# A latent-attention encoder layer on one core: gates of a folded weight and sums of normalised rows are moved to the steps that hold the value products

## The chip, the cores and the metric

The kernel runs on one core of a Trainium2 chip, as one launch. The metric is the time of the launch on the device in microseconds (us). Three runs of the kernel before took 2022.31, 2024.96 and 2029.78 us, with a median of 2024.96 us. One further execution was recorded by the hardware profiler. It took 2024.07 us.

The engines are named as in the profile: PE multiplies matrices, PEld loads its weights, DVE and POOL are the two vector engines, ACT computes activations and copies, SP issues transfers (SPq is its queue).

## The reference

One encoder layer is applied to two sequences of 1024 rows by 1024 columns, `prompt` and `sample`, each with its own conditioning vector. Everything is float32.

```
mod = silu(c) @ w_ada + b_ada            # shift, scale, gate for both halves
h   = rmsnorm(x, g_mix) * (1 + sc1) + sh1
z   = h @ w_in                           # 256 query latents, 128 kv latents, 64 rope, 512 Fourier
p   = softmax((q_nope k_nope + q_pe k_pe) / sqrt(192));  o = p v      # 4 heads
mix = concat(o, fourier(f_in)) @ w_out
x   = x + ga1 * mix
h2  = rmsnorm(x, g_ffn) * (1 + sc2) + sh2
y   = rmsnorm(x + ga2 * ((silu(h2 @ w_gate) * (h2 @ w_up)) @ w_down), g_final)
```

The output is y for both sequences.

## The kernel before

Every product that must keep float32 precision is made of three matmuls: each operand is split into a high part (`hi`, a rounded copy made by ACT, line 63) and a low part (`lo = x - hi`, made by DVE, line 64), and `mm3` (lines 79 to 81) adds hi*hi, hi*lo and lo*hi. So a tensor can be used by PE only after one ACT and one DVE instruction have split it.

The program runs in stages: projections of both sequences into latents and Fourier inputs, a Fourier stage, the attention stage (from 300 to about 716 us in the profile), and the feed-forward stage, which fills the rest. The change lies in the attention stage only.

**The steps.** The attention stage is a loop over k = 0 to 63, one step for each of 2 sequences (s), 4 blocks of 256 rows (b), 4 heads (h) and 2 halves (u) of a block. Steps 0 to 31 belong to sequence 0, steps 32 to 63 to sequence 1. Step k issues:

- `scores` (line 1221): ten matmuls into a PSUM pair, DVE's row maximum `mx` (line 1238), ACT's exponential into `p` (line 1243), DVE's reciprocal and the scaling of `p` (line 1245). The 64 rows of line 1238 in the profile are the 64 steps, and the one numbered k is the start of step k's softmax.
- in steps with k % 8 = 3 and 4, `rope_q` (line 849) for the next block of rows: matmuls, three DVE products `qt` (lines 860 to 862), one POOL sum (863), and the copies `qsk` by ACT and DVE (865, 866).
- in steps with k % 4 = 1 from 5 on, `values` (line 1261): 24 matmuls of the probabilities of four earlier steps with the kv latents, and one split of the result.
- `flip_p` (line 1249) of step k - 1: PE transposes `p` into two PSUM banks `ppt` (line 1258), and ACT and DVE split each bank into `pt`. PE can write a bank again only when both have read it.
- from step 10 to 57, `out_step` (line 1204) for a block finished earlier. Every second step adds an output projection `out_proj` (line 1170) of 12 matmuls against the folded weight `wv`, with a DVE sum (1177). Of each eight, two steps (k % 8 = 4 and 0) end with `norm2` (line 1179). That is a root mean square by ACT (1185), a chain of six small POOL instructions (104 to 111) and a DVE scaling `xn` (1187). Two steps transpose the normalised rows (`flip_h`) and store them to `h2_d`.
- at its end, whatever stands in the table `todo[k]` (lines 1310 to 1328).

**What stands in the table.** The output projection needs the folded weight `wv`, multiplied by the gate `ga1` of the sequence. It is 4 heads by two halves of 512 columns, so eight tiles of 128 x 512. `wv_load` loads them raw. `wv_gate(i)` (line 1299) multiplies tile i by the gate on POOL, in place. `wv_split(i)` (line 1304) splits it on ACT and DVE into `wv`. Tiles 0 to 3 are the first half of the columns, tiles 4 to 7 the second. `gate_half` loads 512 columns of the gate, in a tile with one buffer. So the second half's gate can be loaded only when tiles 0 to 3 are multiplied. All this is done twice: for sequence 0 before step 10 (first half) and step 12 (second half), and for sequence 1 before steps 42 and 44, once sequence 0's last projections are done.

`comb_h(0, c)` (line 1278), for c = 0 to 3, loads four 128 x 512 tiles of sequence 0's normalised rows into `hca`, makes four sums and differences of them on POOL into `hcb`, and stores those to `hc_d` for the feed-forward stage. `hca` and `hcb` have one buffer each. `add_x(i)` (line 821) issues a transfer from POOL's queue that adds a piece of x to a partial result in DRAM. Ahead of it a tiny POOL sum (827) waits for the reciprocal of the step.

**What sets the order.** The program text gives the order of importance. The framework's planner then orders each engine's queue from its own estimate of when each instruction is ready, and an instruction written later can be queued ahead of one that is not ready. The text pins an instruction behind another one on the same engine with `tc.issue_after`. `wv_gate` and `comb_h` are pinned behind `here["p"]`, which is the last POOL instruction of the latest `rope_q` or `norm2` written before. `wv_split` is pinned by `behind()` to the latest split written before. Loads are not pinned: the load for the first combination is written in step 49, whose maximum starts at 617.09 us, and it was issued at 584.28 us. The hardware then runs each queue in order, each instruction when what it waits for has happened.

Of the kernel before, what the change touches and what calls it, by code (L numbers as in the profile page):

```python
# [53 lines left out]
def hybrid_encoder_kernel(ctx: ExitStack, tc: tile.TileContext, a: dict):  # L54
# [7 lines left out]
    def split(hi, lo, src, eng=None):  # L62
        here["a"] = nc.scalar.copy(hi, src).ins  # L63
        here["v"] = (eng or nc.vector).tensor_tensor(out=lo, in0=src, in1=rd(hi), op=ALU.subtract).ins  # L64
# [6 lines left out]
    def behind():  # L71

        st = ExitStack()
        st.enter_context(tc.issue_after(here["a"]))
        st.enter_context(tc.issue_after(here["v"]))
        return st
# [841 lines left out]
    with ExitStack() as st:  # L918
# [180 lines left out]
        for s in range(2):  # L1099
            for t in range(8):  # L1100
# [26 lines left out]
                if s == 0:  # L1127
# [7 lines left out]
                    if t in (4, 6):  # L1135
                        c = t // 2 - 2
# [78 lines left out]
    with ExitStack() as st:  # L1215
# [58 lines left out]
        def gate_half(s, g):  # L1274
            S["ga"] = e.tile([P, 512], F32, tag="gah", name="gah")
            nc.sync.dma_start(S["ga"], ga_d[32 * g + s, :].partition_broadcast(P))

        def comb_h(s, c):
            A = e.tile([P, 4, 512], F32, tag="lat00", name="hca")
            B = e.tile([P, 4, 512], F32, tag="lat01", name="hcb")  # L1280
            for i in range(2):
                nc.sync.dma_start(A[:, 2 * i : 2 * i + 2, :], h2_d[s][:, c + 4 * i, :].rearrange("p (a b) -> p a b", a=2))
            a11, a21, a12, a22 = (A[:, i, :] for i in range(4))
            with tc.issue_after(here["p"]):
                add(B[:, 0, :], a21, a22, nc.gpsimd)
                sub(B[:, 1, :], B[:, 0, :], a11, nc.gpsimd)
                sub(B[:, 2, :], a11, a21, nc.gpsimd)
                sub(B[:, 3, :], a12, B[:, 1, :], nc.gpsimd)
                nc.gpsimd.dma_start(hc_d[s][:, c], B)
# [9 lines left out]
        def wv_gate(i):  # L1299
            h, g = i % 4, i // 4  # L1300
            with tc.issue_after(here["p"]):
                nc.gpsimd.tensor_tensor(out=S["wv", h, g], in0=S["wv", h, g], in1=S["ga"], op=ALU.mult)

        def wv_split(i):
            h, g = i % 4, i // 4
            gs = slice(512 * g, 512 * g + 512)
            with behind():
                split(wv[0][:, h, gs], wv[1][:, h, gs], S.pop(("wv", h, g)))

        todo = {k: [] for k in range(nit)}  # L1310
# [5 lines left out]
                todo[33].append(lambda: gate_half(1, 0))  # L1316
            todo[33 + g].append(lambda g=g: wv_load(1, g))
        for i in range(8):
            todo[39 + i // 2].append(lambda i=i: wv_split(i))
            todo[34 + i // 2].append(lambda i=i: wv_gate(i))  # L1320
            todo[(4, 4, 5, 5, 6, 6, 7, 7)[i]].append(lambda i=i: wv_gate(i))
            if i == 3:
                todo[5].append(lambda: gate_half(0, 1))
                todo[35].append(lambda: gate_half(1, 1))
            todo[6 + i // 2].append(lambda i=i: wv_split(i))
        for c, k in enumerate((49, 51, 57, 59)):
            todo[k].append(lambda c=c: comb_h(0, c))
        for i, k in enumerate((6, 8, 10, 12, 17, 18, 19, 25, 26, 27, 33, 34, 35, 41, 42, 43)):
            todo[k].append(lambda i=i: add_x(i))
# [3 lines left out]
        for k in range(nit + 4):  # L1333
            if k >= nit:
                i = k - nit
# [7 lines left out]
            if k < nit:  # L1343
# [3 lines left out]
                i = k % 8  # L1347
# [657 lines left out]
```

## Time and profile before

| | |
|---|---|
| runs, us | 2022.31, 2024.96, 2029.78 |
| median of the runs, us | 2024.96 |
| profiled execution, us | 2024.07 |
| span of its instructions, us | 2022.3 |
| PE busy in the span, us | 1972.9 (98%) |
| DVE / ACT / POOL busy, us | 1390.8 / 891.4 / 827.1 |
| mean granted clock of PE | 0.997 |
| attention stage, 300 to 716 us: PE busy of 416.00 us | 410.35 |

The span runs from the first to the last instruction of the profiled execution; its time is 1.77 us longer. A row of a timeline gives the start of an instruction in us from the start of the span, its duration in us, the engine, the line of the program, the operation, the tile written and the tiles read, shapes, and in brackets how long the engine was idle before it and what ended that. Where a row has a count over 1 at its end, the duration is that of the whole group. A row of a table by stretches gives, for each engine, busy time and instructions in brackets, then PE's clock, the share of the DMA engines and GB/s.

### The profile page before, as it was taken

To read this page: it belongs to the slowest core of one execution; us is meant where nothing else is said; L and a number is where in the kernel's file an instruction comes from. 1 tells how busy PE (TensorE), PEld (TensorE's weight loads), DVE (VectorE), ACT (ScalarE), POOL (GpSimd) and SP (SyncE) were. 2 spreads that over 40 slices of the span, in tenths; PEclk is the share of its full clock that TensorE was granted. 3 is DMA by queue.
4 is the path that set the end of the run, shared out by engine and by line. 5 is a ranking of instruction groups with operands and counts; after the bars stand their busy time and mean duration, and the time that the engine had idled before them with its cause. 6 is when DMAs were issued, how large, how long until landed. Compare 5 with 4: busy or idle time off the path is not lost.

```text
span 2022.3 us, 27551 instructions
## 1 busy us (share of the span) xinstructions
PE 1972.9 (98%) x9526; PEld 1618.1 (80%) x9526; DVE 1390.8 (69%) x2060; ACT 891.4 (44%) x1716; POOL 827.1 (41%) x972
## 2 busy tenths in 40 slices
PE   6899999999999999999999999999999999999998
PEld 3788778888888877888888888877888888888876
DVE  4568758666777679678778587688655655657674
ACT  2675436555565564333333365453333333336451
POOL 0564212111413237878878411234544544410142
PEclk9999999999999999999999999999999999999999
DMA  9786884445544376555555597674322322358662
GB/s 386 268 320 208 288 311 108 128 91 137 128 115 146 136 265 207 184 187 193 183 180 193 163 312 250 224 229 156 135 88 100 119 91 103 113 186 280 217 224 94
DMA packets 183033, 376.59 MB, mean 186 GB/s; under 512 B 17996, under 2 KB 57548, under 8 KB 179052
## 3 DMA queue, kind: packets, MB, share of 16 engines
q1 hardware_dynamic: 165548, 321.33, 47.1%
q0 software_dynamic: 17344, 53.49, 9.2%
q8 instruction: 75, 1.23, 0.3%
q14 instruction: 66, 0.54, 0.1%
HBM read 262.75 MB, written 120.39 MB: 189 GB/s over the span
## 4 chain that ended last, share of the span: by engine, by line
PE 55%; DVE 3%; DMA 2%; issue 1%; POOL 1%; ACT 0%; SPq 0%; DVEq 0%; ACTq 0%; POOLq 0%
PE bank L80 18%; PE bank L79 18%; PE bank L81 18%; DVE wl L64 1%; DVE val L139 1%; DMA draw<-t_d 1%; DMA draw<-s_d 0%; DMA val<-x_d 0%; DVE val L1802 0%; POOL val L139 0%; ACT wh L63 0%; DVE val L136 0%; POOL rs_y L107 0%; DMA draw<-in_w_down_dram 0%; DVE H L64 0%
## 5 line engine op out<-in xcount | busy, mean ns | idle before, releaser
L79 PE MATMUL bank<-H,wh 128*128 128x512 f32 x1232 | 480.6, 390 | 4.4 <-DVE val L1682 2.2
L80 PE MATMUL bank<-H,wh 128*128 128x512 f32 x1232 | 480.1, 390 | 0.3 <-DVE H L64 0.3
L81 PE MATMUL bank<-H,wl 128*128 128x512 f32 x1232 | 479.8, 390 | 0.2 <-DVE wl L64 0.2
L79 PEld LDWEIGHTS bank<-H,wh 128*128 128x128 f32 x1232 | 231.5, 188 | 55.4 <-DVE val L1682 3.1
L81 PEld LDWEIGHTS bank<-H,wl 128*128 128x128 f32 x1232 | 231.7, 188 | 48.6 <-DVE wl L64 0.5
L80 PEld LDWEIGHTS bank<-H,wh 128*128 128x128 f32 x1232 | 231.6, 188 | 48.2 <-DVE H L64 0.6
L64 DVE TENSOR_TENSOR wl<-draw,wh 128x512 fp32r<-128x512 f32 x286 | 200.9, 738 | 88.9 <-ACT wh L63 88.1
L139 DVE TENSOR_TENSOR val<-bank,val 128x512 f32<-128x512 f32 x200 | 136.6, 689 | 151.9 <-PE bank L81 150.0
L63 ACT CAST wh<-draw 128x512 fp32r<-128x512 f32 x286 | 168.4, 619 | 158.3 <-PE bank L80 86.5
L80 PE MATMUL bank<-wl,wh 128*128 128x512 f32 x572 | 223.6, 391 | 3.5 <-DVE wl L64 3.5
L139 POOL TENSOR_TENSOR val<-val 128x512 f32<-128x512 f32 x58 | 82.0, 1422 | 353.7 <-DVE val L1776 187.6
L79 PE MATMUL bank<-wh 128*128 128x512 f32 x572 | 222.6, 389 | 0.0
L81 PE MATMUL bank<-wh,wl 128*128 128x512 f32 x572 | 222.6, 389 | 0.0
L63 ACT CAST wh<-rgu 128x512 fp32r<-128x512 f32 x172 | 107.1, 622 | 259.9 <-PE bank L80 206.8
L63 ACT CAST wh<-val 128x512 fp32r<-128x512 f32 x133 | 82.3, 622 | 258.3 <-PE bank L80 241.5
L64 DVE TENSOR_TENSOR wl<-val,wh 128x512 fp32r<-128x512 f32 x133 | 128.1, 965 | 69.7 <-ACT wh L63 69.6
L64 DVE TENSOR_TENSOR wl<-rgu,wh 128x512 fp32r<-128x512 f32 x172 | 167.6, 975 | 4.2 <-ACT wh L63 4.2
L136 POOL TENSOR_TENSOR val<-rgu 128x512 f32<-128x512 f32 x80 | 112.1, 1402 | 95.6 <-DMA rgu<-in_wgu_dram 82.3
L80 PEld LDWEIGHTS bank<-wl,wh 128*128 128x128 f32 x572 | 107.3, 188 | 29.0 <-DVE wl L64 6.7
L81 PEld LDWEIGHTS bank<-wh,wl 128*128 128x128 f32 x572 | 107.4, 188 | 22.1
L79 PEld LDWEIGHTS bank<-wh 128*128 128x128 f32 x572 | 107.4, 188 | 22.2
L136 POOL TENSOR_TENSOR val<-val 128x512 f32<-128x512 f32 x89 | 118.8, 1351 | 1.3
(392 smaller groups left out, 3862.3 us busy)
## 6 DMA issues: line engine op xcount, KB each, us to landing
rgu<-in_wgu_dram SPq DMA_DIRECT2D x86, 512.0 KB, 4.4
draw<-s_d SPq DMA_DIRECT2D x143, 256.0 KB, 3.9
s_d<-val POOLq DMA_DIRECT2D x88, 256.0 KB, 3.9
draw<-t_d SPq DMA_DIRECT2D x88, 256.0 KB, 4.2
s_d<-val SPq DMA_DIRECT2D x66, 256.0 KB, 2.7
draw<-in_w_down_dram SPq DMA_DIRECT2D x55, 256.0 KB, 4.2
wada<-in_w_ada_dram SPq DMA_DIRECT2D x11, 1024.0 KB, 10.5
xt<-in_x_dram SPq DMA_DIRECT2D x16, 512.0 KB, 10.3
```

The lines of the kernel that those rows point to most:

```text
L63: here["a"] = nc.scalar.copy(hi, src).ins
L64: here["v"] = (eng or nc.vector).tensor_tensor(out=lo, in0=src, in1=rd(hi), op=ALU.subtract).ins
L79: nc.tensor.matmul(out, lh, rh, start=first, stop=False, skip_group_check=cont)
L80: nc.tensor.matmul(out, lh, rl, start=False, stop=False, skip_group_check=cont)
L81: here["t"] = nc.tensor.matmul(out, ll, rh, start=False, stop=last, skip_group_check=cont).ins
L136: return eng.tensor_tensor(out=out, in0=x, in1=y, op=ALU.subtract).ins
L139: eng.tensor_tensor(out=out, in0=x, in1=y, op=ALU.add)
```

## The change

Only entries of the table `todo` are changed.

- **Gates.** For sequence 0, the gates of tiles 0 to 3 go from steps 4 and 5 to step 5, and those of tiles 4 to 7 from steps 6 and 7 to step 9. For sequence 1, the first four go from steps 34 and 35 to step 37, and the last four from steps 36 and 37 to step 41.
- **Loads of the second half of the gate**: from step 5 to 6, and from step 35 to 38.
- **Splits.** Those of tiles 0 to 3 stay (steps 6 and 7, 39 and 40). Those of tiles 4 to 7 go from steps 8 and 9 to 10 and 11 for sequence 0, and from 41 and 42 to 42 and 43 for sequence 1.
- **Combinations of normalised rows**: from steps 49, 51, 57 and 59 to 49, 53, 57 and 61.

The number of instructions and what each computes stay the same.

```diff
@@ -1316,14 +1316,14 @@
                 todo[33].append(lambda: gate_half(1, 0))
             todo[33 + g].append(lambda g=g: wv_load(1, g))
         for i in range(8):
-            todo[39 + i // 2].append(lambda i=i: wv_split(i))
-            todo[34 + i // 2].append(lambda i=i: wv_gate(i))
-            todo[(4, 4, 5, 5, 6, 6, 7, 7)[i]].append(lambda i=i: wv_gate(i))
+            todo[39 + i // 2 + i // 4].append(lambda i=i: wv_split(i))
+            todo[37 + i // 4 * 4].append(lambda i=i: wv_gate(i))
+            todo[5 + i // 4 * 4].append(lambda i=i: wv_gate(i))
             if i == 3:
-                todo[5].append(lambda: gate_half(0, 1))
-                todo[35].append(lambda: gate_half(1, 1))
-            todo[6 + i // 2].append(lambda i=i: wv_split(i))
-        for c, k in enumerate((49, 51, 57, 59)):
+                todo[6].append(lambda: gate_half(0, 1))
+                todo[38].append(lambda: gate_half(1, 1))
+            todo[6 + i // 2 + 2 * (i // 4)].append(lambda i=i: wv_split(i))
+        for c, k in enumerate((49, 53, 57, 61)):
             todo[k].append(lambda c=c: comb_h(0, c))
         for i, k in enumerate((6, 8, 10, 12, 17, 18, 19, 25, 26, 27, 33, 34, 35, 41, 42, 43)):
             todo[k].append(lambda i=i: add_x(i))
```

## The prediction

> **What bounds the kernel now.** I read the page first, then a table by stretches over the attention stage, then timelines of PE, DVE and POOL around the places where PE stands still.
>
> ```profile
> span 2022.3 us, 27551 instructions
> ...
> PE 1972.9 (98%) x9526; PEld 1618.1 (80%) x9526; DVE 1390.8 (69%) x2060; ACT 891.4 (44%) x1716; POOL 827.1 (41%) x972
> ...
> 300.00:716.00 416.00, 410.35 (x2249) 345.47 (x2248) 297.10 (x540) 232.61 (x469) 97.02 (x154) 1.00 0.48 128
> ```
>
> PE is the bound. In the attention stage, the only one touched, PE is idle for 416.00 - 410.35 = 5.65 us, and no matmul is removed. So the gain has a ceiling of a few us, 0.3% of the time. The question is which idle time belongs to the moved work. A table with one row for each turn of eight steps shows it. I cut the turns at the same instruction of each (the end of the output projection ahead of a transpose): steps 16 to 24, 24 to 32, 32 to 40, 40 to 48 and 48 to 56.
>
> ```profile
> 390.64:445.36 54.72, 54.57 (x300) 46.13 (x300) 36.08 (x69) 30.20 (x62) 8.34 (x20) 1.00 0.42 97
> 445.36:500.09 54.73, 54.58 (x300) 46.13 (x300) 36.08 (x70) 30.21 (x62) 8.40 (x20) 1.00 0.48 110
> 500.09:556.64 56.55, 54.96 (x300) 46.14 (x300) 41.13 (x70) 31.30 (x64) 20.71 (x28) 1.00 0.56 141
> 556.64:611.26 54.62, 54.47 (x300) 46.23 (x300) 40.63 (x78) 33.25 (x69) 8.39 (x20) 1.00 0.49 116
> 611.26:667.81 56.55, 54.97 (x300) 46.14 (x300) 39.60 (x70) 30.25 (x62) 17.46 (x24) 1.00 0.39 130
> ```
>
> Each turn has the same 300 matmuls. Three take 54.62 to 54.73 us, mean 54.69. The third and the fifth take 56.55, so 1.86 us more each. These two are the turns in which POOL is busy for 20.71 and 17.46 us rather than 8.4: the first has the gates of sequence 1, the second two combinations. Within each of them PE stands still once:
>
> ```profile
> 528.89 0.93 PE L1258 MATMUL ppt<-ident,p 128*128 128x128 f32 x5 [1.44 <-DVE pt L64]
> ...
> 640.07 1.14 PE L1258 MATMUL ppt<-ident,p 128*128 128x128 f32 x7 [1.43 <-DVE pt L64]
> ```
>
> Both are steps 35 and 51, at the same place of their turn (k % 8 = 3): PE wants to transpose probabilities, and DVE has not yet emptied the bank. The reason stands in the rows of DVE and POOL just before, against step 43, which has the same work and no POOL sums beside it:
>
> ```profile
> 525.32 1.50 DVE L1245 TENSOR_SCALAR p<-p,rr 128x1024 f32<-128x1024 f32 x1
> 526.74 1.50 DVE L866 TENSOR_TENSOR qsk<-qt,qsk 128x256 fp32r<-128x256 f32 x1
> 528.16 1.28 DVE L64 TENSOR_TENSOR pt<-ppt,pt 128x512 fp32r<-128x512 f32 x2
> ...
> 581.76 0.79 DVE L1245 TENSOR_SCALAR p<-p,rr 128x1024 f32<-128x1024 f32 x1
> 582.47 0.41 DVE L866 TENSOR_TENSOR qsk<-qt,qsk 128x256 fp32r<-128x256 f32 x1
> 582.79 1.28 DVE L64 TENSOR_TENSOR pt<-ppt,pt 128x512 fp32r<-128x512 f32 x2
> ...
> 636.49 1.50 DVE L1245 TENSOR_SCALAR p<-p,rr 128x1024 f32<-128x1024 f32 x1
> 637.92 1.50 DVE L866 TENSOR_TENSOR qsk<-qt,qsk 128x256 fp32r<-128x256 f32 x1
> ```
>
> ```profile
> 524.98 2.98 POOL L1302 TENSOR_TENSOR wvr<-wvr,gah 128x512 f32<-128x512 f32 x2
> ...
> 636.15 1.29 POOL L139 TENSOR_TENSOR hcb<-hca 128x512 f32<-128x512 f32 x1
> ```
>
> With POOL's sums running, the scaling of p takes 1.50 instead of 0.79 us and qsk 1.50 instead of 0.41: 0.71 + 1.09 = 1.80 us, which is the 1.86 us of the turn within its reading. The split of pt, whose first input is in PSUM, is 1.28 in both. DVE runs without a pause through this part of the turn, so what it loses PE loses.
>
> **The change, part by part.**
>
> *Gates of sequence 1.* The first four leave the places where `here["p"]` had put them (two behind step 32's norm, two at 524.98 behind step 35's rope sum) and stand behind step 36's norm, where the last four run now. The last four go behind step 40's norm, at about 564.5.
>
> ```profile
> 537.54 5.95 POOL L1302 TENSOR_TENSOR wvr<-wvr,gah 128x512 f32<-128x512 f32 x4
> ```
>
> ```profile
> 537.63 1.76 DVE L1187 TENSOR_SCALAR xn<-x,rs_r 128x1024 f32<-128x1024 f32 x1 [0.99 <-POOL rs_r L111]
> ...
> 539.83 1.27 DVE L1245 TENSOR_SCALAR p<-p,rr 128x1024 f32<-128x1024 f32 x1
> 542.40 0.69 DVE L64 TENSOR_TENSOR o1b<-gb,o0b 128x512 fp32r<-128x512 f32 x1 [1.30 <-ACT o0b L63]
> ...
> 564.55 0.75 DVE L1187 TENSOR_SCALAR xn<-x,rs_r 128x1024 f32<-128x1024 f32 x1
> ...
> 566.04 0.78 DVE L1245 TENSOR_SCALAR p<-p,rr 128x1024 f32<-128x1024 f32 x1
> 569.27 0.69 DVE L64 TENSOR_TENSOR o1b<-gb,o0b 128x512 fp32r<-128x512 f32 x1 [2.45 <-ACT o0b L63]
> ```
>
> Step 37's row shows what four gates cost in a step with value products: xn takes 1.76 instead of 0.75, p 1.27 instead of 0.78, 1.5 us together, and DVE still idles 1.30 us after it, since PE has 24 value matmuls to make. At step 41 the idle time is 2.45 us, more than 1.5. So the new places cost nothing, and the turn of steps 32 to 40 loses 1.86 us. Bounds: 0 if another stall takes its place, 1.86 if none; I take 1.86 because the DVE difference (1.80) and the turn difference agree. Behind the gates on POOL stands step 41's tiny sum with the transfer that adds x; it starts some 4 us later, and its result is read by the loads of steps 60 and 61, twenty steps on.
>
> *Second combination, 51 to 53.* It goes from behind step 51's rope sum to behind step 52's norm, at about 649.
>
> ```profile
> 650.21 0.75 DVE L1245 TENSOR_SCALAR p<-p,rr 128x1024 f32<-128x1024 f32 x1
> 653.57 0.69 DVE L64 TENSOR_TENSOR o1b<-gb,o0b 128x512 fp32r<-128x512 f32 x1 [2.61 <-ACT o0b L63]
> ```
>
> Here 2.61 us of idle DVE follow: cover enough. The turn of steps 48 to 56 loses another 1.86 us, with the same bounds. The transfers around it: `hca` comes free some 13 us later, so the third combination's load does too. If that load kept its place in SP's queue, it would hold back the store and the load that follow:
>
> ```profile
> 653.12 0.32 SPq L1167 DMA_DIRECT2D x<-fo_d  x1
> ```
>
> ```profile
> 660.31 0.69 DVE L1177 TENSOR_TENSOR x<-x,gb 128x512 f32<-128x512 f32 x1
> ```
>
> That row of x is read first at 660.31, 7 us after the issue, and the combination would end at about 655. Cost 0; at most some 2 us if the load stays ahead.
>
> *Fourth combination, 59 to 61.* Nothing: it waits for its buffer, not for its step.
>
> ```profile
> 691.08 1.28 POOL L139 TENSOR_TENSOR hcb<-hca 128x512 f32<-128x512 f32 x1 [8.80 <-DMA hc_d<-hcb]
> ```
>
> *Gates of sequence 0.* Both fours are pinned behind step 4's rope sum before and after, and POOL has nothing else queued, so I expect them where they are (from 316.87, and from 326.36 when the gate's load has landed), written for steps 5 and 9 or not. Their load moves by a step past nothing in SP's queue. Cost 0.
>
> *Splits of tiles 4 to 7.* Two splits of DVE take 1.28 us:
>
> ```profile
> 356.49 0.69 DVE L1177 TENSOR_TENSOR x<-x,gb 128x512 f32<-128x512 f32 x1 [1.43 <-DMA x<-fo_d]
> ...
> 577.01 1.28 DVE L64 TENSOR_TENSOR wv<-wvr,wv 128x512 fp32r<-128x512 f32 x2
> ...
> 587.63 0.75 DVE L1245 TENSOR_SCALAR p<-p,rr 128x1024 f32<-128x1024 f32 x1
> ...
> 589.84 1.23 DVE L1238 TENSOR_REDUCE mx<-ps_s 128x1 f32<-128x1024 f32 x1 [0.87 <-PE ps_s L1233]
> ```
>
> Step 10's pair fits the 1.43 us of idle DVE. Step 42's pair already stands there. Step 11's and step 43's pairs are new in the crowded part of the turn. `behind()` puts them after the splits of pt, so PE gets its banks as now; what they push by 1.2 us is the maximum of the next step and what follows it, up to the 0.87 us pause ahead of step 45's maximum, and then PE is in value products. I take 0. From above: 0.4 us (1.28 - 0.87) each if PE follows; more only in the third rival below.
>
> The sum: 2024.07 - 1.86 - 1.86 = 2020.4 us against the profiled execution. The median of the runs shown is 0.9 above that execution, which would make it 2021.3. I forecast the middle, 2020.8.
>
> **A rule against it.** The Trainium skill, page "SBUF — State Buffer", section "SBUF: two separate sides", says that DVE (with two SBUF inputs or in a two-port mode) and POOL take a shared port pair as an exclusive lock for a whole instruction, and that the other one waits. The trace agrees in kind: p and qsk, all in SBUF, grow and pt, read from PSUM, does not. By that rule the wait is not removed by moving the gates, it goes to xn and p of steps 41 and 53; the sum by it is the second rival's.
>
> **Rivals.**
> 1. *Half of it.* The planner orders by its own costs, and one of the two stalls reappears, with one gain of 1.86 left: 2022.2. For it: the queues are re-planned. Against: both moved works are pinned behind a norm.
> 2. *The stall moves along.* In steps 41 and 53, xn and p lose 1.5 us as in step 37, and PE feels it: 2024.07 - 3.72 + 2 x 1.5 = 2023.4. Against: step 37's turn has no second stall, and DVE is idle for 2.45 and 2.61 us there.
> 3. *Late splits, slower.* The projections of steps 12 and 44 need the last splits. Step 44's starts here:
>
> ```profile
> 584.54 0.47 PE L79 MATMUL gb<-wv,o0b 128*128 128x512 f32 x1
> ```
>
> Its second half, which needs tiles 6 and 7, is due six matmuls of some 0.23 us later, at about 585.9. If the pair of steps 11 and 43 falls behind the scaling of p (row at 587.63), as step 42's does, it ends at 587.63 + 0.75 + 1.28 = 589.6: PE waits 3.7 us each time, 2020.4 + 7.4 = 2027.8. It is slower than before from 1.9 us each. Against: PE has the next scores to fill in.
> 4. *More.* The other idle time of the stage, 5.65 - 2.87 = 2.78 us, goes too: 2017.6.
>
> **How the numbers follow.** Forecast 0.70, rival 1 0.09, rival 2 0.08, rival 3 0.08, rival 4 0.05. About 0.5% (10 us) is what a measurement of this kernel can tell from no change. No case reaches it; only a re-planning that upsets a later stage would, on either side, and I leave 0.03 for slower and 0.02 for faster. Range: from 2017.6, less the 1.8 us by which the fastest run lies under the profiled one, so 2016, to 2027.8, cut to 2027 for the share of rival 3.
>
> **What would show it.** Right: turns of about 54.7 us everywhere between steps 16 and 56; p and qsk at 0.79 and 0.41 us in steps 35 and 51; xn near 1.76 in steps 40 and 52 with no idle PE after it; gates of sequence 0 where they were. Wrong: an idle PE ahead of line 1258 in another step, or ahead of lines 79 to 81 on `wv` near steps 12 and 44, or turns still at 56.5.

## The result and the profile after

22 runs of the changed kernel took 2019.47 to 2029.52 us, with a median of 2023.27 us. 22 runs of the kernel before took 2022.31 to 2032.35 us, with a median of 2027.52 us. The ratio is 0.9983, with a 95% interval from 0.9975 to 0.9990. Times 2027.52 us that is a gain of 3.4 us, between 2.0 and 5.1; the two medians lie 4.2 us apart, inside the same interval. The sum of the prediction was a gain of 3.7 us. By the bound of 0.5% the kernel is the same; the gain is smaller than that bound, but its interval leaves out no change.

The profiled execution took 2021.37 us, against 2024.07 before. The page and the table by stretches of the attention stage of the kernel after (the columns are those of the table in the prediction):

```profile
span 2019.6 us, 27553 instructions
...
PE 1972.4 (98%) x9526; PEld 1618.4 (80%) x9526; DVE 1387.4 (69%) x2060; ACT 890.3 (44%) x1716; POOL 827.9 (41%) x972
...
302.00:718.00 416.00, 413.24 (x2265) 348.43 (x2264) 297.54 (x542) 233.69 (x471) 98.26 (x158) 1.00 0.48 129
```

In a stretch of 416 us PE is now idle for 2.76 us instead of 5.65. The difference, 2.89, is the two stalls of 1.44 and 1.43 us, 2.87 together. The turns of eight steps, cut at the same instruction as before:

```profile
393.03:447.77 54.74, 54.59 (x300) 46.16 (x300) 36.08 (x69) 30.19 (x62) 8.31 (x20) 1.00 0.42 97
447.77:502.47 54.70, 54.55 (x300) 46.15 (x300) 36.12 (x69) 30.18 (x62) 7.87 (x20) 1.00 0.49 110
502.47:557.17 54.70, 54.56 (x300) 46.16 (x300) 37.63 (x69) 31.16 (x64) 13.82 (x24) 1.00 0.57 146
557.17:611.79 54.62, 54.48 (x300) 46.14 (x300) 42.43 (x77) 32.90 (x69) 14.65 (x24) 1.00 0.47 116
611.79:666.51 54.72, 54.58 (x300) 46.17 (x300) 39.27 (x69) 30.18 (x62) 17.78 (x24) 1.00 0.41 135
```

The third turn fell from 56.55 to 54.70 and the fifth from 56.55 to 54.72: 1.85 + 1.83 = 3.68 us. POOL works as long as before in the fifth turn (17.78 us, 17.46 before), only elsewhere in it. Four gates went from the third turn to the fourth (POOL 14.65 us there, 8.39 before), and the fourth still takes 54.62 us.

The best clock for what follows is the stage itself, from the first score matmul (first start of line 1229) to the last row maximum (last start of line 1238). Before, that is 299.8 to 708.1, or 408.3 us; after, 302.0 to 706.8, or 404.8 us. That is 3.5 us less; the stretch ahead of step 16 took 0.2 us more in this trace (see the run with the splits alone). The start of the stage alone differs between the runs of this study, whose program up to there is the same, from 299.8 to 306.3 us. That is more than the whole effect. So one time of a run says nothing here, and the turns of a trace say it to about 0.1 us. The runs below that were timed once bear this out: they took 2019.39 to 2026.22 us, and the lowest of these times belongs to a run with a longer turn than the changed kernel (the late splits).

### The profile page after: what moved, and what is told of

It reads as the page before. It is cut to its first block, busy times and chain, and to the rows that moved or that the text cites. A ratio compares the mean times of both kernels' runs of the same rounds, so it can differ in the third digit from the quotient of the medians.

```text
span 2019.6 us, 27553 instructions
## 1 busy us (share of the span) xinstructions
PE 1972.4 (98%) x9526; PEld 1618.4 (80%) x9526; DVE 1387.4 (69%) x2060; ACT 890.3 (44%) x1716; POOL 827.9 (41%) x972
## 4 chain that ended last, share of the span: by engine, by line
PE 55%; DVE 3%; DMA 2%; POOL 1%; issue 1%; ACT 0%; SPq 0%; DVEq 0%; ACTq 0%; POOLq 0%
PE bank L80 18%; PE bank L81 18%; PE bank L79 18%; DVE wl L64 1%; DMA draw<-t_d 1%; DVE val L139 1%; POOL val L139 1%; DMA val<-x_d 0%; DVE val L1802 0%; ACT wh L63 0%; DMA X<-hc_d 0%; DMA ga<-ga_d 0%; DVE val L136 0%; POOL rs_y L107 0%; DMA draw<-in_w_down_dram 0%
```

## The experiments

**One part at a time.** The first pair of runs separates the gates from the combinations. In the first, the combinations alone were put back:

```diff
-        for c, k in enumerate((49, 53, 57, 61)):
+        for c, k in enumerate((49, 51, 57, 59)):
```

> The changed kernel with the combinations back in steps 49, 51, 57 and 59; gates and splits stay moved. Theory (POOL's sums beside step 35 and beside step 51 each cost one stall of their own): the turn of steps 32 to 40 stays at 54.7 us, that of steps 48 to 56 returns to 56.55 with 1.4 us of idle PE ahead of line 1258, and the time lies 1.86 us above the changed kernel, 1.86 below the one before. Rival (the gain comes from a re-planned order of the whole stage, not from the place of the sums): the turns do not fall apart into one short and one long, and both lie between 54.7 and 56.5.

In the second, the kernel before got the combinations' new steps alone:

```diff
-        for c, k in enumerate((49, 51, 57, 59)):
+        for c, k in enumerate((49, 53, 57, 61)):
```

> The kernel before with only the combinations moved, to steps 49, 53, 57 and 61. Theory: the mirror of the run with the combinations undone. The turn of steps 32 to 40 stays at 56.55 us with p at 1.50 and qsk at 1.50 us in step 35, the turn of steps 48 to 56 falls to 54.7, the time lies 1.86 us below the kernel before. The fourth combination runs when its buffer is free, as before. Rival (re-planned order): as in the other run, no clean division.

The third and the fifth turn with the combinations back:

```profile
503.55:558.21 54.66, 54.51 (x301) 46.13 (x300) 37.56 (x70) 31.17 (x64) 14.36 (x24) 1.00 0.57 145
612.87:669.39 56.52, 54.96 (x301) 46.14 (x300) 39.59 (x70) 30.25 (x62) 17.45 (x24) 1.00 0.39 130
```

and PE's stall in it, in the timeline of PE:

```profile
641.65 1.04 PE L1258 MATMUL ppt<-ident,p 128*128 128x128 f32 x6 [1.41 <-DVE pt L64]
```

The same turns with the combinations alone moved:

```profile
501.58:558.14 56.56, 54.97 (x300) 46.14 (x300) 41.12 (x70) 31.31 (x64) 20.70 (x28) 1.00 0.54 141
612.75:667.45 54.70, 54.55 (x301) 46.15 (x300) 39.28 (x70) 30.21 (x62) 17.83 (x24) 1.00 0.41 135
```

Each part takes its own turn from about 56.5 to 54.7 us and leaves the other alone. The stage takes 406.4 us in both (303.3 to 709.7, and 301.3 to 707.7), halfway between 408.3 and 404.8. So the two gains add up, and the rival of a re-planned order falls. The times do not contradict this, and could not have decided it: ratios to the kernel before of 0.9995 (0.9983 to 1.0007) and 0.9992 (0.9981 to 1.0002).

**The splits alone.** The kernel before with only the splits moved:

```diff
-            todo[39 + i // 2].append(lambda i=i: wv_split(i))
+            todo[39 + i // 2 + i // 4].append(lambda i=i: wv_split(i))
...
-            todo[6 + i // 2].append(lambda i=i: wv_split(i))
+            todo[6 + i // 2 + 2 * (i // 4)].append(lambda i=i: wv_split(i))
```

> The kernel before with only the splits of tiles 4 to 7 moved, by two steps for sequence 0 and by one for sequence 1. Theory: the two long turns stay at 56.55 us, the turn of steps 40 to 48 at 54.6, and from the stall of step 7 to the cut ahead of step 16 it takes some 0.2 us more than the 53.14 us of the kernel before, as in the changed kernel (53.37). Rival (the split moves are part of the gain): one of the long turns gets shorter by over 0.3 us.

```profile
502.51:559.04 56.53, 54.98 (x300) 46.15 (x300) 41.08 (x69) 31.27 (x64) 20.65 (x28) 1.00 0.54 140
559.04:613.78 54.74, 54.59 (x301) 46.14 (x300) 40.73 (x78) 32.91 (x69) 8.38 (x20) 1.00 0.49 116
613.78:670.32 56.54, 54.94 (x301) 46.14 (x300) 39.62 (x69) 30.22 (x62) 17.45 (x24) 1.00 0.39 130
```

Both long turns stay, so the splits bring none of the gain. What is left of the third turn's gain is the gates, with the load of their second half, which was not run apart from them. The splits cost nothing either. From the first score matmul to the cut ahead of step 16 this run takes 90.8 us, as the kernel before does (90.85); the 0.2 us more that the changed kernel showed (393.03 - 301.96 = 91.07) did not come back, nor did it in the other runs with the changed splits (90.8 to 90.9). My expectation of 0.2 us was the spread between runs.

**How much POOL work, and where.** Three runs add dead work to the changed kernel. It stands in turns that had none, on the gate tile while nobody uses it:

```diff
+        def idle_sums(n):
+            with tc.issue_after(here["p"]):
+                for _ in range(n):
+                    nc.gpsimd.tensor_tensor(out=S["ga"], in0=S["ga"], in1=S["ga"], op=ALU.subtract)
+
+        for k, n in ((19, 1), (27, 4)):
+            todo[k].append(lambda n=n: idle_sums(n))
```

> The changed kernel plus dead POOL work: the gate tile minus itself (128 x 512, two inputs in SBUF), once behind step 19's rope sum and four times behind step 27's, while the tile is not in use. Theory (each of DVE's scaling of p and of qsk waits for the POOL sum that runs when it starts, and PE has no slack there): the single sum catches p alone, p 1.50 and qsk 0.41 us, turn of steps 16 to 24 at 55.4 us (54.7 + 0.7); the four catch both, p and qsk 1.50, turn of steps 24 to 32 at 56.55 with some 1.4 us of idle PE, no more than two sums cost in step 35 before. Rival (DVE's loss grows with the time POOL is busy): four sums cost about 3.7 us. Rival (it was the re-planned order): both turns stay at 54.7.

The turns of steps 16 to 24, 24 to 32 and 32 to 40 of this run:

```profile
391.13:446.27 55.14, 54.91 (x300) 46.14 (x300) 36.52 (x69) 30.30 (x62) 9.73 (x21) 1.00 0.42 96
446.27:502.29 56.02, 54.94 (x300) 46.14 (x300) 37.38 (x70) 30.30 (x62) 12.92 (x24) 1.00 0.47 112
502.29:557.01 54.72, 54.57 (x301) 46.14 (x300) 37.60 (x70) 31.18 (x64) 14.32 (x24) 1.00 0.56 146
```

DVE in step 19, beside one sum, and in step 27, beside four:

```profile
416.35 1.24 DVE L1245 TENSOR_SCALAR p<-p,rr 128x1024 f32<-128x1024 f32 x1
417.51 0.41 DVE L866 TENSOR_TENSOR qsk<-qt,qsk 128x256 fp32r<-128x256 f32 x1
...
471.50 1.24 DVE L1245 TENSOR_SCALAR p<-p,rr 128x1024 f32<-128x1024 f32 x1
472.65 1.26 DVE L866 TENSOR_TENSOR qsk<-qt,qsk 128x256 fp32r<-128x256 f32 x1
```

and POOL beside them (the first two of the four):

```profile
416.00 1.04 POOL L1333 TENSOR_TENSOR gah<-gah 128x512 f32<-128x512 f32 x1
...
471.15 2.48 POOL L1333 TENSOR_TENSOR gah<-gah 128x512 f32<-128x512 f32 x2
```

The pattern is the expected one. One sum catches p alone and the turn grows by 0.44 us (55.14 - 54.70). Four catch p and qsk and no more. The first two end at 473.63 us; the other two run from 474.51 to 476.97, beside the splits of pt, the maximum and the products qt, which read PSUM and keep their time. The turn grows by 1.32 us, where four in proportion to one would be 1.8, and in proportion to POOL's time 3.7 by the rival. The sizes were too high, 0.7 and 1.85 expected, because this sum, with one tile on both inputs, takes 1.04 us and not a gate's 1.30, so it delays p and qsk less. DVE loses 1.24 + 1.26 - 0.78 - 0.41 = 1.31 us and PE 1.32: in this place PE has no slack to be seen.

The same sums behind the norms ahead of the value products:

```diff
+        for k, n in ((21, 4), (29, 8)):
+            todo[k].append(lambda n=n: idle_sums(n))
```

> The changed kernel plus the same dead POOL sums behind the norms ahead of the value products: four behind step 20's norm (written in step 21) and eight behind step 28's (written in step 29). Theory (DVE's idle time in a step with value products covers what xn and p lose): the turn of steps 16 to 24 stays at 54.7 us although xn takes 1.76 and p 1.3 us; with eight, POOL works some 11 us, up to the softmax of the step after, and the turn of steps 24 to 32 is longer by 0.5 us at most. Rival (the place does not matter, only the work): both are longer by 1.5 us or more.

```profile
392.92:447.62 54.70, 54.55 (x301) 46.15 (x300) 37.09 (x70) 30.18 (x62) 13.07 (x24) 1.00 0.43 97
447.62:502.30 54.68, 54.53 (x301) 46.16 (x300) 37.08 (x70) 30.17 (x62) 17.32 (x28) 1.00 0.50 116
```

Eight sums, 9.53 us of POOL, and the turn takes 54.68 us. DVE's rows of step 29 show where they go:

```profile
483.32 1.51 DVE L1187 TENSOR_SCALAR xn<-x,rs_r 128x1024 f32<-128x1024 f32 x1 [0.99 <-POOL rs_r L111]
...
485.26 1.01 DVE L1245 TENSOR_SCALAR p<-p,rr 128x1024 f32<-128x1024 f32 x1
488.08 0.69 DVE L64 TENSOR_TENSOR o1b<-gb,o0b 128x512 fp32r<-128x512 f32 x1 [1.81 <-ACT o0b L63]
```

xn and p take longer, and 1.81 us of idle time are still left before DVE's next instruction. So the place decides, not the amount. The eight sums end at 492.77 us, before p of the next step begins (493.52), so a row of sums that reaches into that step was not tried.

The third run of this kind fills the tile instead, which reads nothing from SBUF:

```diff
+                    nc.gpsimd.memset(S["ga"], 0.0)
...
+        for k, n in ((19, 5), (27, 2)):
```

> The changed kernel plus POOL fills, which write the gate tile and read nothing from SBUF (128 x 512, about 0.55 us each): five behind step 19's rope sum, two behind step 27's. Theory (qsk, with two inputs in SBUF, waits only for a POOL instruction that reads SBUF; the scaling of p, with one input, waits for any): qsk stays at 0.41 us, p grows by at most one fill to 0.8 to 1.35 us, turn of steps 16 to 24 at 54.7 to 55.3. Rival (any POOL instruction makes both wait): qsk grows as well, to 0.7 to 0.95, turn at up to 55.8.

POOL in step 19, then DVE:

```profile
421.96 1.59 POOL L1333 MEMSET gah<- 128x512 f32 x2
```

```profile
422.33 0.75 DVE L1245 TENSOR_SCALAR p<-p,rr 128x1024 f32<-128x1024 f32 x1
423.00 0.42 DVE L866 TENSOR_TENSOR qsk<-qt,qsk 128x256 fp32r<-128x256 f32 x1
```

p and qsk are as in a step without POOL work, and the two turns take 54.70 and 54.72 us. qsk stays, as the theory says; the theory expected p to grow, and it did not. The first fill had nearly ended when p began, so whether p would wait for a whole one is open. The fills take longer instead. The four fills in the kernel before last 545 ns on average:

```profile
L771 POOL MEMSET wnr<- 128x512 f32 x4 | 2.2, 545 | 5.7 <-PE bank L81 4.7 <-DVE wn L1015 1.1
```

The two fills here take 1.59 us, 0.5 more than two of those.

**Late splits.** This run goes further towards the third rival of the prediction, with all four splits in the last step:

```diff
-            todo[39 + i // 2 + i // 4].append(lambda i=i: wv_split(i))
+            todo[39 + i // 2 if i < 4 else 43].append(lambda i=i: wv_split(i))
...
-            todo[6 + i // 2 + 2 * (i // 4)].append(lambda i=i: wv_split(i))
+            todo[6 + i // 2 if i < 4 else 11].append(lambda i=i: wv_split(i))
```

> The changed kernel with all four splits of tiles 4 to 7 in the last step before they are read: 11 for sequence 0, 43 for sequence 1. It tests the third rival of the prediction, late splits. Theory (DVE has no idle time in steps 11 and 43, and the projections of steps 12 and 44 follow at once): four splits take 2.5 us there, of which the 0.87 us pause behind the crowded part and PE's next scores cover a part; the turn of steps 40 to 48 goes from 54.62 to 55.0 to 56.5 us, and the stretch up to the cut ahead of step 16 gets longer by 0.3 to 1.8 us. Rival (the planner fills PE with other work, and late splits are free): both within 0.2 us of the changed kernel.

```profile
582.07 1.28 DVE L64 TENSOR_TENSOR pt<-ppt,pt 128x512 fp32r<-128x512 f32 x2
583.27 2.48 DVE L64 TENSOR_TENSOR wv<-wvr,wv 128x512 fp32r<-128x512 f32 x4
585.67 1.21 DVE L1238 TENSOR_REDUCE mx<-ps_s 128x1 f32<-128x1024 f32 x1
```

```profile
555.81:610.75 54.94, 54.75 (x301) 46.16 (x300) 42.26 (x78) 33.22 (x69) 14.62 (x24) 1.00 0.47 116
```

2.48 us of splits in DVE's most crowded step cost 54.94 - 54.62 = 0.32 us. At step 11 they cost 0.1 us against the changed kernel and 0.3 to 0.4 against the other runs with its splits (91.2 us from the first score matmul to the cut, against 91.07 and 90.8 to 90.9). So the cost lies about where the theory (0.3 us or more) and its rival (0.2 or less) meet. The splits stand behind the ones that empty PE's banks. What they push is the next maximum. Meanwhile PE has twelve matmuls of projection and ten of scores to do (583.82 to 588.93 us). The rival's own condition, splits behind the scaling of p, did not come about here either, so its price of 3.7 us was not tried.

**A version that goes further.** One of the three stalls left in the stage is 0.56 us ahead of line 1231 in step 7. DVE has two of sequence 0's splits in its queue ahead of step 7's maximum. The edit:

```diff
-            todo[6 + i // 2 + 2 * (i // 4)].append(lambda i=i: wv_split(i))
+            todo[8 + i // 2].append(lambda i=i: wv_split(i))
```

> The changed kernel with sequence 0's splits of tiles 0 to 3 in steps 8 and 9 instead of 6 and 7, and those of tiles 4 to 7 in steps 10 and 11 as they are. Theory: the idle 0.56 us of PE ahead of line 1231 in step 7 comes from the two splits (1.28 us) that stand ahead of step 7's maximum in DVE's queue, so it goes, or moves by at most as much to steps 8 and 9; the other turns keep 54.7 us. Rival: the idle time comes from the start of the pipeline and stays at 0.56 us.

PE's waits in the stage, from 300 to 720 us, after:

```profile
PE ps_s L1229 <- ACT qa L63: 0.7, 1, 0.7
PE ppt L1258 <- DVE nb L1239: 0.6, 1, 0.6
PE ps_s L1231 <- DVE nb L1239: 0.6, 1, 0.6
```

and with the splits later:

```profile
PE ps_s L1229 <- ACT qa L63: 0.7, 1, 0.7
PE ppt L1258 <- DVE nb L1239: 0.6, 1, 0.6
```

The stall is gone, the turns keep 54.7, and the stage takes 403.8 us (305.5 to 709.3), 1.0 less than the changed kernel. From the first score matmul to the cut ahead of step 16 it takes 90.1 us, against 90.8 to 91.1 in the other runs with the changed splits, so the gain lies in that stretch. Timed:

> The changed kernel with sequence 0's splits of tiles 0 to 3 in steps 8 and 9, now timed. Expected from the look before it: 1.0 us below the changed kernel, so 4.5 us below the kernel before in the attention stage (403.7 instead of 408.3 us from the first scores to the last maximum); ratio about 0.998. Rival: the other idle times of the stage take it back, and the stage takes 404.8 us as in the changed kernel.

The stage took 404.0 us (300.8 to 704.8), 4.3 under the kernel before. The ratio to the kernel before is 0.9974, with an interval from 0.9963 to 0.9984. That interval too leaves out no change, and by the bound of 0.5% the kernel is again the same. The interval overlaps that of the changed kernel, so by the times the two cannot be told apart; the gain of 0.8 to 1.0 us over it rests on the two traces.

## Why the prediction was right

**The bound and the ceiling.** PE was the bound and stayed it (1972.9 and 1972.4 us busy). But idle PE is not the whole of what a stall costs, and so 5.65 us was no strict ceiling. Of the 3.68 us, 2.87 were idle time; the other 0.8 show as shorter busy time of the same 300 matmuls (54.96 to 54.56 us in the third turn, 54.97 to 54.58 in the fifth). The rows of PE at the stall of step 35 show where that lies, first before, then after:

```profile
527.17 0.28 PE L81 MATMUL gb<-wq_h,ql 128*128 128x256 f32 x1
528.89 1.25 PE L1258 MATMUL ppt<-ident,p 128*128 128x128 f32 x8 [1.44 <-DVE pt L64]
529.90 0.47 PE L79 MATMUL gb<-wv,o0b 128*128 128x512 f32 x1
...
529.53 0.28 PE L81 MATMUL gb<-wq_h,ql 128*128 128x256 f32 x1
529.65 1.05 PE L1258 MATMUL ppt<-ident,p 128*128 128x128 f32 x8
530.45 0.47 PE L79 MATMUL gb<-wv,o0b 128*128 128x512 f32 x1
```

From start to start, PE needs 529.90 - 527.17 = 2.73 us before and 530.45 - 529.53 = 0.92 after. That is 1.81 us less, and DVE's loss was 1.80. The 1.44 us in brackets leaves out the end of the matmul ahead of the gap and the slower transposes behind it. The prediction took the price of a stall from the turns and not from the idle time, and that made its sum come out.

**The two stalls.** Step 35 of the kernel after has p and qsk at their short durations, and DVE runs on into the splits:

```profile
527.67 0.78 DVE L1245 TENSOR_SCALAR p<-p,rr 128x1024 f32<-128x1024 f32 x1
528.38 0.41 DVE L866 TENSOR_TENSOR qsk<-qt,qsk 128x256 fp32r<-128x256 f32 x1
528.71 1.28 DVE L64 TENSOR_TENSOR pt<-ppt,pt 128x512 fp32r<-128x512 f32 x2
```

Step 51 has 0.75 and 0.42. The forecast of 1.86 us for each turn was met with 1.85 and 1.83. That the POOL sums are the cause, and not a new order of the queues that came with the move, was only argued in the prediction. The runs with one part each show it, and so do the dead sums, on a tile that nobody else uses then.

**The new places are free.** The rows of step 41, which has the gates now:

```profile
565.07 1.75 DVE L1187 TENSOR_SCALAR xn<-x,rs_r 128x1024 f32<-128x1024 f32 x1
...
566.92 1.59 DVE L1245 TENSOR_SCALAR p<-p,rr 128x1024 f32<-128x1024 f32 x1
569.78 0.69 DVE L64 TENSOR_TENSOR o1b<-gb,o0b 128x512 fp32r<-128x512 f32 x1 [1.27 <-ACT o0b L63]
```

xn is 1.75, as forecast; p is 1.59 rather than 1.27, so the loss is 1.8 instead of 1.5 us. The idle time behind it shrank from 2.45 to 1.27 and still covers it. Beside the second combination, xn takes 1.75 and p 1.26 us, and 1.34 of 2.61 us of idle time are left. The second rival, the stall that moves along, falls. The wait that the Trainium skill states ("SBUF — State Buffer", section "SBUF: two separate sides") agrees with these longer xn and p; it now falls on instructions that PE is not waiting for.

**What was not moved by being moved.** The gates of sequence 0 run at 319.0 us, 17.1 us after the first score matmul, as before (316.9 and 299.8). The fourth combination waits for its buffer exactly as before:

```profile
689.79 1.29 POOL L139 TENSOR_TENSOR hcb<-hca 128x512 f32<-128x512 f32 x1 [8.80 <-DMA hc_d<-hcb]
```

The third combination's load did not hold up SP's queue: the planner put it behind the load of x (issued at 649.26 and 653.48 us).

**Where the working was off.** Besides the ceiling, two steps of it were wrong, without harm to the sum. Step 10's pair of splits was said to fit the 1.43 us of idle DVE. It does not stand there: the sum that waits for x came first in DVE's queue, and the splits follow behind it.

```profile
358.22 0.69 DVE L1177 TENSOR_TENSOR x<-x,gb 128x512 f32<-128x512 f32 x1 [1.46 <-DMA x<-fo_d]
358.83 0.16 DVE L1244 RECIPROCAL rr<-sm 128x1 f32<-128x1 f32 x1
358.90 0.67 DVE L64 TENSOR_TENSOR wv<-wvr,wv 128x512 fp32r<-128x512 f32 x1
```

An idle time at the head of which a waiting instruction stands is not free for what is queued behind it. And the third rival's case did not arise. It supposed the pair of step 43 behind the scaling of p; the planner put it right behind the bank splits, where it ends at 585.9 us, and the products that need it begin at 586.6. Even four splits there cost no more than 0.4 us.

**The level.** The forecast of 2020.8 us started from three runs with a median of 2024.96; 22 runs gave 2027.52, and the kernel after came out at 2023.27, inside the range. The difference was right. The level was 2.5 us low because the median of the first three runs lay low in a spread of 10 us. That the time fell inside the range says little: 2024.96 us, the kernel before by those three runs, lies inside it too. The turns carry the proof.

## What to carry to other kernels

Where one engine is busy for 98% of the time, cut the trace into turns of the loop with equal work and compare their lengths: a turn that is longer than its like shows the price and the place of a stall to 0.1 us, when the time of a run scatters by several. A side job on POOL costs by what DVE is doing beside it: it was free, even eight sums long, where PE had a long run of products and DVE idle time behind it, and cost its full delay where DVE ran without a pause into the instruction that releases PE's buffer. The same holds within DVE's own queue: 1.8 us ahead of that instruction cost 1.86 us, and 2.5 us behind it cost at most 0.4.

## What the runs showed of the hardware that was not expected

- The loss of DVE beside POOL did not grow with POOL's work. What counted was how many DVE instructions with operands in SBUF met a sum: one sum met p and cost the turn 0.44 us; of four, two met p and qsk, and the four cost 1.32. None of those shown here lost more than 1.09 us (qsk, 0.41 to 1.50), less than one sum of 1.30.
- A POOL sum that reads one tile on both inputs took 1.04 us, one that reads two tiles 1.30 (both 128 x 512, float32).
- Fills by POOL did not slow qsk (0.42 us beside one that ran), nor p (0.75) where it began as a fill was about to end; the two fills took 1.59 us, 0.5 more than two undisturbed ones.
